# A two-layer hybrid trunk in float32: the S5 mixer's output products issued for two steps together, in four column groups

## The chip, the cores and the metric

The kernel runs on one core of a Trainium2 chip. The metric is the device time of one execution in microseconds (us), the median of three runs. A program that reads the hardware profile gives one profiled execution as a trace; its times count from the start of its span.

## The reference

One sequence of 256 positions, width 2048, two layers. Each layer normalises, scales and shifts by a modulation vector, projects to four head groups, mixes, projects back, and adds with a gate; then an MLP with squared ReLU.

```python
mod = c_act @ ada_w[l] + ada_b[l]
sh1, sc1, gt1, sh2, sc2, gt2 = split(mod, 6)
a = rms_norm(h, norm1_g[l]) * (1 + sc1) + sh1
proj = a @ w_in[l]                      # columns of S5, retention, window, latent attention
mixed = concat([y_s5, y_ret, y_swa, y_mla]) @ w_out[l]
h = h + gt1 * mixed
a = rms_norm(h, norm2_g[l]) * (1 + sc2) + sh2
h = h + gt2 * (square(relu(a @ mlp_w1[l])) @ mlp_w2[l])
```

The S5 mixer has 32 groups of 16 channels and 64 complex modes each: a linear recurrence over the positions, then

```python
y = einsum('bsgp,ghp->bsgh', st_r, c_re) - einsum('bsgp,ghp->bsgh', st_i, c_im) + d_skip * uf
z = gelu(y)
return z * sigmoid(z @ glu_w + glu_b)
```

## The kernel before, in words

Weights arrive as a stream of items of 256 rows by 512 columns (a few are narrower) by DMA on SyncE's queue (`pump_dma`, line 324). Each item is split into a high and a low part: ScalarE casts it to `wH`, VectorE makes the rest `wL` (`prep`, line 335). TensorE makes three products for each pair of tiles, high by high, high by low and low by high, so an item is 12 to 24 instructions. A list (`make_plan`, line 82) sets the order of the items; the items of the modulation (`ap`) go to TensorE directly, as products of 32 columns in four column groups (`pe_ap`, line 456).

The mixers run in the background of that stream. Each is a Python generator (`s5` at line 1310, `mla` for latent attention at 908, `swa` for the window at 858, `ret` for retention at 1054). After each piece of an item `step` (line 395) lets them advance in turn until what they emitted in this step is above a share of an engine's time (`BUD`, line 238), counted by estimates; S5 goes first. A generator that needs tiles or banks of PSUM waits until enough are free (`g_slots`, line 277, and `g_banks`), with 31 tiles and 8 banks in all. All engines take their instructions in the order in which this code emits them. All products stand under line 225 in the trace, since a helper records them, so the names of tiles tell them apart: `w<-` and `p<-` are general tiles and banks.

S5 takes its 16 sets of 128 modes two at a time, in eight steps `p`. A step reads the input's products from two banks, turns them into a rotating frame, scans both halves of the sequence on VectorE, and turns the states back: four results for each of two sets, in the tiles `W[2]` and `W[3]`. Then eight output products follow: four terms (real and imaginary part, two frames) for each of the two sets `e`. A product is 128 modes by 32 channels on 256 positions, and the 32 channels of set `i` stand in column group `32 * (i % 4)` of the bank `yp`. Two steps fill the four column groups of a bank, an even step the first two and an odd step the other two; then VectorE adds the skip term.

At the head of the output product `hload` and `ysplit` (line 708) wait for latent attention, the first of the four mixers that the output product takes, by `need`: the generators go on with no item of the stream between them until it is done.

```python
P8 = W[2 + e].rearrange("p c (b t) -> p (c b) t", b=2)   # line 1396
...
yield from g_slots(4)                                     # line 1326
```

Of the kernel before, what the change touches and what calls it, by code (L numbers as in the profile page):

```python
# [36 lines left out]
# blocks of the first layer's input product that run in step over k while the modulation arrives  # L37
EARLY = ("U", "C", "K", "Q")
# order of the other blocks, and of the mixers' outputs (s5, retention, window, latent) in the output product
# [27 lines left out]
def _gap(l, f):  # L67
    """the norm ahead of a block, with products of the modulation to fill the tensor engine's wait"""
    g = _ap_sec(l, SH1 if f == 1 else SH2, [2, 3])
    p = g[:8] + [("sqfin",)] + g[8:13] + [("norm", l, f)]  # L70
    if f == 1:
        p += [("start", l), ("lim", 6, 3)]
    p.append(("aquad", l, f, 0))
    return p + g[13:] + [("crepfree",)]


# halves of a quad of the normed input, ahead of which item of the block they are made
# [102 lines left out]
# columns of the constant array  # L180
# [30 lines left out]
class Meter:  # L211
    """An engine whose emitted work is counted, so that background work can be spread evenly."""
# [18 lines left out]
def trunk_kernel(ctx: ExitStack, tc: tile.TileContext, A, out):  # L231
    nc = tc.nc
    V, ACT, GP = Meter(nc.vector, 0.07, 1.04e-3), Meter(nc.scalar, 0.12, 0.83e-3), nc.gpsimd
    PE = Meter(nc.tensor, 0.05, 1.5e-3)

    NHL, NS, LA = 3, 31, 4
    # work that each slot of the stream may bring in, in us of vector, scalar and tensor engine, by layer
# [123 lines left out]
    def prep_real():  # L361
        """the next item that the scalar and vector engines prepare"""
# [5 lines left out]
    # items behind the next norm are not prepared ahead of it  # L368
    wall, w, k = {}, len(data_idx), len(data_idx)
    for it in reversed(PLAN):  # L370
# [3 lines left out]
        elif it[0] == "norm":  # L374
            w = k
# [19 lines left out]
    def step():  # L395
        """one slot: background generators advance until the slot's share of an engine is used up"""
# [84 lines left out]
    def ap_cols():  # L481
        """the row of 512 sums, four partial sums to a column, turned into four columns"""
# [29 lines left out]
    nst = {"acc": None, "pb": None}  # L512

    def sq_add(sq, w):
        """adds the squares of w chunks to the running sum over features"""
# [7 lines left out]
    def sq_fin():  # L523
        """the sum over partitions"""
# [30 lines left out]
    def aquad_a(l, f, q):  # L555
        """a = rstd * h * g * (1 + scale) + shift in two parts, the shortest way to the first chunks"""
# [23 lines left out]
    def aquad_half(l, f, q, c, stage):  # L580
        """the same for two chunks, in three stages that run apart"""
# [31 lines left out]
    def fm(acc, n, k0, first, last, xH, xL, w=512, wo=0, ng=4):  # L613
        """acc[bank][:, 256*...] += W.T @ x over the two k-chunks of item n; x as four-chunk tiles."""
# [39 lines left out]
    def pe_in(n, it):  # L654
        _, l, b, kq, hf = it
        # at the start, with all blocks in progress at once, two of them are summed up in SBUF
# [61 lines left out]
    def evict_half(l, gate, nb, acc, b):  # L718
        """h += gate * acc for two chunks, as soon as their bank is complete"""
# [100 lines left out]
    def softmax4(pv, sv, mask, scale, sink):  # L820
        """sv = softmax over the free axis of scale * (pv + mask), with an optional sink logit"""
# [20 lines left out]
    def transposed(views, nk):  # L842
        """[128 keys, 4 heads, 128 queries] per block of keys"""
# [796 lines left out]
```

## Time and profile before

| | |
|---|---|
| three runs | 2373.75, 2376.07, 2376.28 us |
| median | 2376.07 us |
| the profiled execution | span 2373.1 us; no other time of it is kept |
| instructions | 42933 |
| granted TensorE clock, mean | 0.991 of full speed |
| TensorE busy | 2303.7 us, 97% |
| VectorE busy | 1523.9 us, 64% |
| ScalarE busy | 1038.2 us, 44% |

Busy times are sums over the whole span; stages differ. The median of the runs is 3.0 us above the profiled span. The first layer's mixers stand between about 170 and 410 us, the second layer's between about 1290 and 1540 us. A product's row in the timeline has the time from its start until its end as modelled; products overlap, so the distance between starts is what one costs TensorE. The chain of waits follows the work that ended last back from its end.

### The profile page before, as it was taken

Reading aid. Unit: us, or ns where it says so; the run is one execution under the profiler, and the core shown is the slowest. Engines: PE = TensorE matmul, PEld = TensorE weight load, DVE = VectorE, ACT = ScalarE, POOL = GpSimd, SP = SyncE. Lnnn points to the kernel's source line nnn. Section 1 sums busy time; section 2 is a strip of 40 time slices with the busy share of each in tenths; the row PEclk is TensorE's granted clock in tenths of the full one; section 3 lists DMA queues with packets and bytes.
Section 4 is the critical chain, followed back from the end, with each engine's and each line's share of the span. In section 5 each row is a group of like instructions: output and inputs, shape, how many; then the busy total and the mean of one; then the engine's idle time right before and its main releaser. Section 6 shows DMA issues by size and latency. Waiting matters only on the chain.

```text
span 2373.1 us, 42933 instructions
## 1 busy us (share of the span) xinstructions
PE 2303.7 (97%) x17610; PEld 2092.8 (88%) x17610; DVE 1523.9 (64%) x2532; ACT 1038.2 (44%) x1330; POOL 31.8 (1%) x51
## 2 busy tenths in 40 slices
PE   6999999999999999999999889999999999999997
PEld 3675457989999999999988757898999999999997
DVE  4847774666666677788877986576444445555555
ACT  2343234554444444434445346445444444343444
POOL 0000000000000000000000000000000000000000
PEclk9999999999999999999999999999999999999999
DMA  9985786777888889988976224877555556676730
GB/s 379 408 309 190 272 305 262 249 286 258 273 275 282 273 295 322 319 320 284 323 278 245 98 69 145 299 269 289 183 201 182 194 191 211 238 233 231 237 126 36
DMA packets 161077, 583.65 MB, mean 246 GB/s; under 512 B 18240, under 2 KB 18400, under 8 KB 160880
## 3 DMA queue, kind: packets, MB, share of 16 engines
q1 hardware_dynamic: 156240, 563.80, 67.2%
q0 software_dynamic: 4640, 17.11, 2.0%
q8 instruction: 138, 2.26, 0.4%
q14 instruction: 59, 0.48, 0.1%
HBM read 576.64 MB, written 4.19 MB: 245 GB/s over the span
## 4 chain that ended last, share of the span: by engine, by line
PE 90%; DVE 5%; DMA 3%; ACT 1%; issue 1%; SPq 0%; POOL 0%; DVEq 0%; POOLq 0%; ACTq 0%
PE p L225 90%; DVE w L225 3%; DMA w<-in_stream_dram 3%; DVE wL L225 1%; ACT wH L225 0%; ACT w L225 0%; DVE s5i L225 0%; DVE nacc L225 0%; DVE aL L225 0%; ACT aH L225 0%; POOL mss L925 0%; SPq L306 0%; DVE ndg L225 0%; ACT L225 0%; ACT apev L225 0%
## 5 line engine op out<-in xcount | busy, mean ns | idle before, releaser
L225 PE MATMUL p<-aH,wH 128*128 128x256 f32 x4896 | 1393.7, 285 | 8.6 <-ACT aH L225 5.4
L225 PE MATMUL p<-aH,wL 128*128 128x256 f32 x4896 | 1388.3, 284 | 3.2 <-DVE wL L225 3.2
L225 PE MATMUL p<-aL,wH 128*128 128x256 f32 x4896 | 1388.3, 284 | 1.8 <-DVE aL L225 1.8
L225 DVE TENSOR_TENSOR wL<-w,wH 128x1024 fp32r<-128x1024 f32 (+1 forms) x688 | 833.4, 1215 | 734.9 <-ACT wH L225 723.1
L225 ACT CAST wH<-w 128x1024 fp32r<-128x1024 f32 (+1 forms) x688 | 712.5, 1039 | 928.5 <-PE p L225 845.5
L225 PEld LDWEIGHTS p<-aH,wH 128*128 128x128 f32 x4896 | 942.2, 192 | 25.4 <-ACT aH L225 7.8
L225 PEld LDWEIGHTS p<-aH,wL 128*128 128x128 f32 x4896 | 942.2, 192 | 3.8 <-DVE wL L225 3.8
L225 PEld LDWEIGHTS p<-aL,wH 128*128 128x128 f32 x4896 | 942.3, 192 | 2.6 <-DVE aL L225 2.4
L225 PE MATMUL p<-w,w 128*32 128x512 f32 (+5 forms) x1464 | 251.2, 508 | 12.3 <-DVE w L225 10.1
L225 DVE CUSTOM_DVE_ANT_0 w<-w,w 128x1024 f32<-128x1024 f32 x192 | 233.8, 1218 | 0.0
L225 PEld LDWEIGHTS p<-w,w 128*32 128x32 f32 (+3 forms) x1464 | 97.8, 134 | 110.0 <-issue 57.5
L225 PE MATMUL p<-wH,aH 128*128 128x512 f32 (+1 forms) x320 | 128.4, 401 | 5.9 <-ACT wH L225 5.9
L225 PE MATMUL p<-wL,aH 128*128 128x512 f32 (+1 forms) x320 | 118.9, 372 | 0.5 <-DVE wL L225 0.5
L225 PE MATMUL p<-wH,aL 128*128 128x512 f32 (+1 forms) x320 | 118.5, 370 | 0.0
L225 PEld LDWEIGHTS p<-wH,aH 128*128 128x128 f32 x320 | 60.8, 190 | 43.6 <-issue 22.1
L225 ACT ACTIVATE w<-w 128x1024 f32<-128x1024 f32 (+3 forms) x82 | 67.1, 823 | 55.1 <-DVE w L225 50.2
L225 ACT COPY w<-p 128x512 f32<-128x512 f32 (+1 forms) x80 | 45.6, 586 | 101.5 <-PE p L225 100.3
L225 DVE TENSOR_TENSOR aL<-w,aH 128x1024 fp32r<-128x1024 f32 (+2 forms) x86 | 72.2, 847 | 12.9 <-ACT aH L225 12.9
L225 PEld LDWEIGHTS p<-wH,aL 128*128 128x128 f32 x320 | 60.8, 190 | 11.0
L225 DVE TENSOR_TENSOR w<-w,w 128x512 f32<-128x512 f32 (+4 forms) x132 | 65.9, 526 | 6.2 <-ACT w L225 4.0
L225 PEld LDWEIGHTS p<-wL,aH 128*128 128x128 f32 x320 | 60.9, 190 | 9.8 <-DVE wL L225 1.4
L225 ACT ACTIVATE w<-p 128x512 f32<-128x512 f32 x68 | 40.6, 598 | 43.6 <-PE p L225 43.5
(153 smaller groups left out, 786.8 us busy)
## 6 DMA issues: line engine op xcount, KB each, us to landing
w<-in_stream_dram SPq DMA_DIRECT2D x1056, 512.0 KB, 4.9
w<-in_stream_dram SPq DMA_DIRECT2D x16, 320.0 KB, 9.5
w<-in_w_uq_dram POOLq DMA_DIRECT2D x6, 384.0 KB, 6.1
w<-in_xT_dram SPq DMA_DIRECT2D x4, 512.0 KB, 7.4
w<-in_glu_w_dram POOLq DMA_DIRECT2D x4, 512.0 KB, 5.6
w<-in_xT_dram POOLq DMA_DIRECT2D x4, 512.0 KB, 7.4
w<-in_c_dram POOLq DMA_DIRECT2D x4, 512.0 KB, 6.6
hs<-w POOLq DMA_DIRECT2D x4, 512.0 KB, 3.9
```

The lines of the kernel that those rows point to most:

```text
L225: return f(out, *a, **k)
```

## The change

S5 holds six tiles instead of four: the results of an even step go to `W[2]` and `W[3]`, those of an odd step to `W[4]` and `W[5]`. An even step emits no output products. The odd step takes a bank and emits the sixteen products of both steps: for each of the four terms the four sets, which go to four column groups. The rest of the text's difference is comments that were left out.

```diff
-        yield from g_slots(4)
-        W = [slot([128, 4, 256]) for _ in range(4)]
+        yield from g_slots(6)
+        W = [slot([128, 4, 256]) for _ in range(6)]
...
-                P8 = W[2 + e].rearrange("p c (b t) -> p (c b) t", b=2)
+                P8 = W[2 + 2 * (p % 2) + e].rearrange("p c (b t) -> p (c b) t", b=2)
...
-            if p % 2 == 0:
+            if p % 2 == 1:
+
                 yield from g_banks(1, 1)
                 yp = bank()
-            for n, (m, src) in enumerate(((0, 0), (0, 3), (1, 2), (1, 1))):
-                for e in range(2):
-                    i = 2 * p + e
-                    p0, cs, o = 32 * (i % 4), slice(32 * i, 32 * i + 32), 256 * (n == 3)
-                    PE.matmul(yp[p0:p0 + 32, o:o + 256], lhsT=C[:, m, cs], rhs=W[2 + e][:, src, :],
-                              start=n in (0, 3), stop=n in (2, 3), tile_position=(0, p0))
-            if p % 2 == 1:
+                for n, (m, src) in enumerate(((0, 0), (0, 3), (1, 2), (1, 1))):
+                    for e in range(4):
+                        i = 2 * p - 2 + e
+                        p0, cs, o = 32 * e, slice(32 * i, 32 * i + 32), 256 * (n == 3)
+                        PE.matmul(yp[p0:p0 + 32, o:o + 256], lhsT=C[:, m, cs], rhs=W[2 + e][:, src, :],
+                                  start=n in (0, 3), stop=n in (2, 3), tile_position=(0, p0))
                 yield
```

Since tiles, banks and counted time decide where each generator goes on, the other mixers' instructions move too. Three places show it. First TensorE in the first layer, ahead of the first output product. Before, the last products of S5's gate, the window's sums (`64x512`) and transposes of softmax results stand there:

```order
L225 MATMUL p_3107<-w_3153,w_110 32x512 x2
L225 MATMUL p_3107<-w_3157,w_110 32x512 x2
L225 MATMUL p_3257<-kc,apev 128x1 x4
L225 MATMUL p_3272<-w_3186,w_1516 64x512
L225 MATMUL p_3272<-w_3193,w_1516 64x512
L225 MATMUL p_3276<-kc,w_3059 128x128 x4
L225 MATMUL p_3283<-kc,w_3097 128x128 x2
L225 MATMUL p_3283<-kc,w_3098 128x128 x2
```

With the change, some rows after the scores of the second half of latent attention, these rows stand there (`w_3083` and `w_3084` are the retention queries and keys, `w_3107` and `w_3108` softmax results of the window):

```order
L225 MATMUL p_3241<-kc,apev 128x1 x4
L225 MATMUL p_3236<-w_3078,w_3074 128x256 x2
L225 MATMUL p_3236<-w_3078,w_3075 128x256 x2
L225 MATMUL p_3261<-kc,w_3083 128x128 x4
L225 MATMUL p_3285<-kc,w_3083 128x128 x4
L225 MATMUL p_3298<-w_3084 128x256
L225 MATMUL p_3298<-w_3084 128x128
L225 MATMUL p_3303<-kc,w_3107 128x128 x2
L225 MATMUL p_3303<-kc,w_3108 128x128 x2
L225 MATMUL p_3308<-w_3084 128x256
L225 MATMUL p_3308<-w_3084 128x128
```

The scores of latent attention and all of retention's heads have come ahead of the first output product; before, the scores stood among the input products and the heads among the output products.

Second, ScalarE's queue at the same place, with the change (`sxd` and `sxm` are sums and maxima of a softmax, `w_3209` and `w_3210` scores of latent attention):

```order
L225 ACTIVATE w_1477<-p_3236,s5d 128x256 x2
L225 COPY w_3084<-p_3261 128x4x128
L225 ACTIVATE w_3107<-w_3107,sxd 128x256 x2
L225 ACTIVATE w_3108<-w_3108,sxd 128x256 x2
L225 ACT_TABLE_LOAD
L225 ACTIVATE w_3209,sxd<-w_3209,sxm 128x256 x2
L225 ACTIVATE w_3210,sxd<-w_3210,sxm 128x256 x2
L225 COPY w_3084<-p_3285 128x4x128
L225 ACTIVATE w_3209<-w_3209,sxd 128x256 x2
L225 ACTIVATE w_3210<-w_3210,sxd 128x256 x2
L225 COPY w_3328<-p_3303 128x512
```

and before, where the queue ends in the cast of latent attention's result (`aH`):

```order
L225 ACTIVATE w_3097<-w_3097,sxd 128x256 x2
L225 ACTIVATE w_3098<-w_3098,sxd 128x256 x2
L225 COPY w_1712<-p_3272 64x4x128
L225 COPY w_3281<-p_3276 128x512
L225 COPY w_3288<-p_3283 128x512
L225 COPY w_3295<-p_3290 128x512
L225 COPY w_2803<-p_3297 128x4x128
L225 COPY w_2803<-p_3303 128x4x128
L225 CAST aH_3324<-w_2803 128x1024
```

A softmax of latent attention, with its table load, now stands between the two copies of the retention queries.

Third, TensorE in the second layer, inside the input product of the window's queries, with the change:

```order
L225 MATMUL p_14043<-aL_13291,wH 128x256
L225 MATMUL p_14043<-aH_13290,wL 128x256
L225 MATMUL p_14243<-w_13284,w_14149 128x256
L225 MATMUL p_14243<-w_13285,w_14149 128x256
L225 MATMUL p_14243<-w_13286,w_14149 128x256
L225 MATMUL p_14042<-aH_13375,wH 128x256
L225 MATMUL p_14042<-aL_13376,wH 128x256
```

Before, the same three products of latent attention's queries stand in the product of the retention queries, 180 instructions of the stream later:

```order
L225 MATMUL p_14398<-wH,aL_13481 128x512
L225 MATMUL p_14710<-w_14598,w_13736 64x512
L225 MATMUL p_14715<-w_13282,w_14208 128x256
L225 MATMUL p_14715<-w_13283,w_14208 128x256
L225 MATMUL p_14715<-w_13284,w_14208 128x256
L225 MATMUL p_14397<-wH,aH_13480 128x512
```

The other five groups of three, the key and value products and the first scores of latent attention have moved with them.

## Rows read from the trace of the kernel before

**Rows 1.** The page: span and instructions, and busy time of each engine.
```profile
span 2373.1 us, 42933 instructions
...
PE 2303.7 (97%) x17610; PEld 2092.8 (88%) x17610; DVE 1523.9 (64%) x2532; ACT 1038.2 (44%) x1330; POOL 31.8 (1%) x51
```
**Rows 2.** Chain that ended last, 170 to 420: start, us, what, instructions.
```profile
292.68 84.15 PE p L225 x434
...
385.28 1.05 ACT aH L225
...
387.64 32.48 PE p L225 x253
```
**Rows 3.** The same chain, 1280 to 1520.
```profile
1392.10 107.66 PE p L225 x506
...
1500.39 1.28 ACT L225
```
**Rows 4.** Busy time by stretch: length, busy by engine, granted clock, DMA share, GB/s.
```profile
1295.00:1392.00 97.00, 80.15 (x532) 62.98 (x531) 85.94 (x240) 35.26 (x68) 3.35 (x3) 0.95 0.23 79
1392.00:1500.00 108.00, 107.90 (x508) 77.74 (x509) 76.02 (x179) 57.90 (x115) 4.22 (x8) 1.00 0.43 153
293.00:371.00 78.00, 78.00 (x409) 43.40 (x406) 49.62 (x140) 32.04 (x65) 1.06 (x2) 0.97 0.71 258
1380.00:1390.00 10.00, 7.24 (x19) 4.63 (x20) 6.48 (x22) 4.55 (x11) 0.00 (x0) 0.51 0.15 52
```
**Rows 5.** Timeline, one burst of S5's output products: start, us, engine, instructions.
```profile
307.63 0.40 PE L225 MATMUL p<-wH,aL 128*128 128x512 f32 x1
...
307.96 1.44 PEld L225 LDWEIGHTS p<-w,w 128*32 128x32 f32 x16 [0.36 <-issue]
307.96 1.92 PE L225 MATMUL p<-w,w 128*32 128x256 f32 x16
...
309.81 0.50 PE L225 MATMUL p<-wH,aH 128*128 128x512 f32 x1
```
**Rows 6.** Timeline, the modulation's products: two items together, and one alone.
```profile
350.74 1.06 PE L225 MATMUL p<-w,w 128*32 128x512 f32 x8
...
356.75 1.05 PE L225 MATMUL p<-w,w 128*32 128x512 f32 x4
```
**Rows 7.** Timeline, other mixers on TensorE: scores, gate, column sums, a retention head.
```profile
352.36 0.70 PE L225 MATMUL p<-krT,w 64*128 64x256 f32 x2
352.99 0.70 PE L225 MATMUL p<-w,w 128*128 128x256 f32 x2
...
360.59 1.89 PE L225 MATMUL p<-w,w 128*128 128x256 f32 x8
...
377.49 1.05 PE L225 MATMUL p<-kc,apev 128*128 128x1 f32 x8 [0.73 <-ACT apev L225]
...
1513.21 0.92 PE L225 MATMUL p<-w 64*128 64x256 f32 x4
```
**Rows 8.** Timeline, TensorE's first products behind the first layer's input product.
```profile
370.95 5.80 PE L225 MATMUL p<-w,w 128*128 128x256 f32 x32
```
**Rows 9.** ScalarE: one exponential, table load, four scalings (timeline), and copies (by form).
```profile
360.36 0.49 ACT L225 ACTIVATE w<-w,sxm 128x256 f32<-128x256 f32 x1
...
361.95 1.28 ACT L225 ACT_TABLE_LOAD   x1
...
378.06 1.70 ACT L225 ACTIVATE w<-w,sxd 128x256 f32<-128x256 f32 x4
...
L225 ACT COPY w<-p 128x512 f32<-128x512 f32 x72 | 40.9, 587 | 89.1 <-PE p L225 87.9 <-DVE aL L225 0.6
```
**Rows 10.** Timeline, the second layer's product after a long wait of TensorE.
```profile
1380.22 0.79 PE L225 MATMUL p<-wH,aH 128*128 128x512 f32 x1 [5.91 <-ACT wH L225]
```
**Rows 11.** Timeline, three products of latent attention's queries and the one behind them.
```profile
1407.89 1.46 PE L225 MATMUL p<-w,w 128*128 128x256 f32 x6
1408.99 0.58 PE L225 MATMUL p<-wH,aH 128*128 128x512 f32 x1
```

## The prediction

> **What bounds the kernel now.** I read the page first, then the chain of work that ended last in the two stretches that hold an S5 mixer, then the busy time by stretch, then single bursts in the timeline. The page [rows 1]: TensorE is busy 97% of a span of 2373.1 us. A kernel like this gets shorter only by TensorE work that disappears or by TensorE idle time that closes. The chains say where TensorE is the limit. In the first layer it carries the chain for 84.15 us from 292.68, and after one ScalarE cast at 385.28 again from 387.64 [rows 2]; between 267 and 292.7 the chain is VectorE's. In the second layer TensorE has it for 107.66 us from 1392.10 and hands over at 1500.39 to a table load [rows 3]; ahead of that, from 1295, VectorE has it. The stretches agree [rows 4]: from 1295 to 1392 VectorE is busy 85.94 of 97 us and TensorE only 80.15, from 1392 to 1500 TensorE 107.90 of 108 and VectorE 76.02; from 293 to 371 TensorE 78.00 of 78, VectorE 49.62. So TensorE time saved between 1295 and 1392 buys nothing, saved behind 1392 or behind 293 it is the kernel's.
>
> **The change, part by part.** *The bursts.* One S5 step issues 8 output products, 16 instructions, to two column groups. In the timeline [rows 5] the 16 start at 307.96 and the next product of the stream at 309.81; the last product before started at 307.63. Products of that stream follow at 0.23 us, so a burst costs 309.81 - 307.63 - 0.23 = 1.95 us. 1.85 us for 16 instructions is about eight steps of 0.216: two instructions share a step already. Four groups are seen elsewhere: the modulation's products write 32 columns each too, and eight of their instructions (two items, four column groups) take 1.06 us, four (one item, two groups) 1.05 us [rows 6]. Twice the groups, same time. Those stream 512 columns, the S5 products 256, so I take 0.216 us for a set of four and 1.95 us for a burst of 32. Bounds: 1.95 (as with the modulation) and 3.7 (no gain over pairs, 32 instructions at two to a step and one change of form). Sixteen bursts become eight: 8 x 1.95 = 15.6 us of TensorE work less.
>
> A row that bears on the weights: the 16 loads of that burst are spread over 1.44 us at the same time as its products [rows 5], although all use the same 128 rows. The Trainium skill (TensorE: Matmul & The Clock Gate, Part 3, "What overlaps and what doesn't") says that a load overlaps running products only when the row group differs; by that rule these loads would stand between the products. The row speaks against it, and by it a burst of 32 would cost 2.9 us more (32 loads at 1.44/16).
>
> *What else moves.* The work of the mixers is dealt out in steps by emitted engine time, with slots and banks as tokens. S5 now wants 6 tiles instead of 4, an even step emits no products, and the bank of the sums is held inside the odd step only. The order shows what follows: in both layers S5 keeps its pace, but the latent and retention work lands elsewhere. I sum TensorE time by place, with prices from rows: a score product every 0.63 us, so a block of eight 5.0, half a gate product of S5 (four products) 1.89, column sums 1.05, one retention head 0.92 [rows 7]. Small scores are half as wide, 0.4 each and 3.2 a block, by an estimate from the same rows.
>
> *First layer.* (a) Up to the last quarter of the retention queries the work is 1 us more, in VectorE's stretch: 0. (b) From there to the end of the input product (288 to 371) four bursts become two (-3.9), the latent scores of the second half (-5.0) go behind it, half a gate product too (-1.9), and small scores, a wide product and transposes (an estimate of 4.4) go ahead of it: -15. VectorE, busy near its limit up to 340, keeps some: I take **-13** (bounds -6 and -15).
>
> (c) Then the output product must wait for latent attention. Before, the time from the last input product's end to the first output product is 370.95 [rows 8] to the end of the cast, 386.3 [rows 2]: 15.4 us. Now the second half's scores stand inside it. I follow the order by durations. TensorE: gate half 1.9, modulation 1.0, scores 5.0, modulation 1.0, gate half 1.9, column sums 1.05, gate half 1.9: 13.7. ScalarE, in its queue: two sigmoids (0.9), copy 0.59, four scalings 1.70, table 1.28, four exponentials of 0.49, and only then the copy of the second half of the retention queries, 0.59 [rows 9]: 20.8. All retention heads wait for that copy, and TensorE idles from 14.4 to 20.8. Then four heads 3.7, sixteen transposes and the products of three mixers behind them, an estimate of 7.4: 32. A copy, four squares and the cast (1.05) [rows 2] close it: about 35 us. Difference **+20**. The rows also show what such an idle time does to the clock: after TensorE had stood idle for 5.91 us up to 1380.22 [rows 10], the granted clock from 1380 to 1390 was 0.51 [rows 4], the lower of its two levels (1.2 GHz), and the product at 1380.22 took 0.79 us. I add **+2** for that (bounds 0 and 5). (d) Retention's heads and output products, which stood inside the output product, have moved ahead: **-6.9** (four heads 3.4 to 3.7, small products 2.8, transposes 0.7, the last two by estimate). First layer: -13 + 20 + 2 - 6.9 = **+2**.
>
> *Second layer.* The latent projections move ahead by some 20 weight items, from TensorE's stretch into VectorE's: six groups of three products, each 1.1 us (1407.89 to 1408.99) [rows 11], and by estimate from such rates transposes 1.0, key and value products 2.8, small scores 3.2: 13.7 us. (e) 1295 to 1392: TensorE gets +13.7 and loses three bursts, 5.9; its 17 us of idle time take the 7.8. VectorE gets six operations of the queries' rotary, an estimate of 2.2 us: **+2.7** with what the tighter coupling costs (bounds 0 and 10). (f) 1392 to 1500: -13.7, one burst less (-1.95), three to four retention heads come in (+3.4): **-12.2**. TensorE then needs 96 us against VectorE's 78, so it stays the bound. (g) Behind 1505 those heads and small products are gone: **-5.0**. The end at 1500 (table, two activations, cast) does not hang on latent attention and stays. Second layer: 2.7 - 12.2 - 5.0 = **-14.5**.
>
> DMAs: no transfer is added or taken out; two more tiles held by S5 delay some weight issues by one item, which the prefetch covers except perhaps between 325 and 371, inside (b)'s bound. VectorE's and ScalarE's instructions are the same in number but for one table load.
>
> Sum: +2 - 14.5 = **-12.5 us** on the span of 2373.1. The median of the runs, 2376.07, is 3 us above that span; the same difference on it gives **2364 us**. A measurement of this kernel can tell about 0.2%, 4.75 us, from no change.
>
> **Rivals.**
> *Only the bursts count* (0.20): the delay (c) is hidden or (b) comes in full, and the two layers net to the 15.6 us less work, a little more where idle time closes: 2360. For it: TensorE is busy 97%. Against: one third of the bursts stand in VectorE's stretches.
> *VectorE holds both stretches* (0.12), the slower side: in the first layer VectorE (or the weights' DMA) does not let the input product end earlier, so (b) gives 4 instead of 13, while (c) costs its 20 to 22; in the second the 7.8 us in (e) come on top of VectorE's chain. Sum: -4 + 22 - 6.9 + 10 - 12.2 - 5.0 = +4, and +9 if (f) also loses half to VectorE: 2377 to 2385. It decides from the point where (b) is below 7. For it: VectorE is at 89% from 1295 on [rows 4]. Against: 49.62 of 78 from 293 on.
> *The groups do not overlap by fours* (0.07): each burst keeps two to a step, 1.75 us more on the six bursts outside VectorE's stretch, -12.5 + 10.5 = -2: 2374. Against it: rows 6.
> *The loads are exposed* (0.03): 2.9 us more on six bursts, 2381. It is what the rule of the skill quoted above would do here; the trace does not agree with that rule.
>
> **How the numbers follow.** The forecast's own case has 0.58; the likeliest time is its 2364, its own range 2354 to 2373 (drain (c) as little as 27 us, TensorE's work alone, gives -8; (b), (e) and the clock at their bad ends give +9). Low end: 2353, just under that. High end: 2376, which takes in the third rival and leaves out most of the second and the fourth, some 0.15, and 0.05 lie under the low end. Faster by over 0.2%: 0.48 of the first, 0.20 of the second, 0.01 of the groups' case: 0.69. Within 0.2%: 0.08 + 0.07 + 0.06: 0.21. Slower: 0.02 + 0.05 + 0.03: 0.10.
>
> **What the profile after would show.** Eight bursts of 32 instructions that start in sets of four, 0.22 us apart, 1.8 to 2.0 us each. In the first layer the last input product ends near 358, the first output product starts near 393, with some 6 us of idle TensorE ahead of the first retention head, named as waiting for ScalarE. In the second layer the chain leaves VectorE near 1397 and the stretch to the output product is about 12 us shorter. I am wrong if pairs are seen in the bursts, if the first layer's output product starts later than 400, or if VectorE keeps the chain of the second layer beyond 1410.

## The result and the profile after

The change makes the kernel slower: 2395.8 us (median of 2393.88 to 2404.28) against 2375.47 us, with a recorded ratio of 1.0092 and a 95% interval of 1.0079 to 1.0105. The forecast was 2364, in a range of 2353 to 2376.

The page after, beside [rows 1]:

```profile
span 2395.7 us, 42934 instructions
...
PE 2306.0 (96%) x17610; PEld 2100.2 (88%) x17610; DVE 1523.9 (64%) x2532; ACT 1040.7 (43%) x1331; POOL 30.9 (1%) x51
```

TensorE has the same 17610 instructions and is busy 2.3 us *longer*, although sixteen bursts have become eight. Its idle time is 2395.7 - 2306.0 = 89.7 us, and was 69.4.

A burst where nothing waits, from TensorE's timeline after (start, us, engine, instructions):

```profile
1365.71 1.93 PE L225 MATMUL p<-w,w 128*32 128x256 f32 x32
1367.57 0.39 PE L225 MATMUL p<-aH,wH 128*128 128x256 f32 x1
```

32 instructions hold TensorE from 1365.71 to 1367.57, 1.86 us; 16 took 1.85 [rows 5]. Their weights load at the same time:

```profile
1365.70 1.45 PEld L225 LDWEIGHTS p<-w,w 128*32 128x32 f32 x32
```

Where nothing waits, the part that the change is about does what was forecast. Four of the eight bursts are like this one: their first and last starts lie 1.55 us apart. In the other four these starts lie 2.36 (first layer), 7.33, 7.41 and 6.11 us apart (second layer). These bursts wait in their middle for results of VectorE, and those of the second layer then run at the lower clock; two of them are shown below.

The first layer's drain, TensorE's timeline after, to be read against [rows 2, 8] (the last figure is the idle time and what ended it):

```profile
364.71 3.51 PE L225 MATMUL p<-w,w 128*128 128x256 f32 x18
...
385.00 1.64 PE L225 MATMUL p<-w 64*128 64x256 f32 x4 [5.98 <-ACT w L225]
...
404.12 0.38 PE L225 MATMUL p<-aH,wH 128*128 128x256 f32 x1 [3.34 <-ACT aH L225]
```

and ScalarE in it:

```profile
379.38 1.71 ACT L225 ACTIVATE w<-w,sxd 128x256 f32<-128x256 f32 x4
381.12 1.28 ACT L225 ACT_TABLE_LOAD   x1
...
384.39 0.56 ACT L225 COPY w<-p 128x512 f32<-128x512 f32 x1
```

The first retention head (385.00) waits 5.98 us for the copy of the second retention queries, which stands behind four scalings, a table load and four exponentials. Behind that wait TensorE has the lower of its two clock levels, 0.50 of full speed (columns as in [rows 4]):

```profile
385.00:394.00 9.00, 8.99 (x34) 7.13 (x35) 2.40 (x8) 3.16 (x8) 0.00 (x0) 0.50 0.02 2
```

The first output product starts at 404.12, before at 386.3.

The chain after, where the input product of the first layer should have come sooner (start, us, what):

```profile
296.62 3.48 DMA w<-in_stream_dram
...
326.05 7.10 DMA w<-in_stream_dram
333.23 1.05 ACT wH L225
334.30 1.23 DVE wL L225
...
343.27 34.89 PE p L225 x187
```

Before, TensorE had the chain without a break from 292.68 [rows 2]. Now two weights arrive late, 10.6 us of the chain, and TensorE has it for good only from 343.27.

The second layer, busy time by stretch after; the columns are those of [rows 4]:

```profile
1412.00:1526.00 114.00, 100.22 (x463) 69.44 (x462) 77.14 (x182) 55.09 (x103) 3.68 (x7) 0.96 0.46 166
```

Before, the same part of the stream, from 1392 to 1500, had TensorE busy 107.90 of 108 [rows 4]. It lost its latent projections, as forecast, and takes longer: 13.8 us are idle. The waits of TensorE in it:

```profile
PE p L225 <- DVE w L225: 8.3, 3, 4.0
PE p L225 <- ACT w L225: 5.2, 3, 3.4
```

One of the three waits for VectorE, in the timeline of all engines:

```profile
1425.75 0.41 ACT L225 ACTIVATE w<-w,sxm 128x128 f32<-128x128 f32 x1 [5.11 <-DVE sxm L225]
...
1427.10 0.63 PE L225 MATMUL p<-w,w 128*32 128x256 f32 x6
...
1428.83 1.03 ACT L225 CAST wH<-w 128x1024 fp32r<-128x1024 f32 x1
...
1429.89 1.22 DVE L225 TENSOR_TENSOR wL<-w,wH 128x1024 fp32r<-128x1024 f32 x1 [2.28 <-ACT wH L225]
...
1431.04 1.28 DVE L225 TENSOR_TENSOR w<-w,w 128x512 f32<-128x512 f32 x2
...
1431.78 3.37 PE L225 MATMUL p<-w,w 128*32 128x256 f32 x26 [4.04 <-DVE w L225]
...
1435.07 0.77 PE L225 MATMUL p<-wH,aH 128*128 128x512 f32 x1
```

The stretch behind the wait (columns of [rows 4]), then the second layer's last burst in TensorE's timeline:

```profile
1431.80:1435.00 3.20, 3.20 (x26) 1.08 (x26) 1.66 (x2) 0.10 (x1) 0.00 (x0) 0.57 0.60 193
...
1470.44 0.63 PE L225 MATMUL p<-w,w 128*32 128x256 f32 x6
1473.57 3.42 PE L225 MATMUL p<-w,w 128*32 128x256 f32 x26 [2.50 <-DVE w L225]
```

Read the first of the two views from its end. The burst stops after 6 of 32 instructions, because VectorE has not made the last set's results (1431.04). These stand behind the low part of a weight (1429.89), that waited 2.28 us for ScalarE's cast (1428.83), the cast stands behind latent attention's small exponentials (1425.75), and these waited 5.11 us for VectorE's maxima. Three queues in order, each waiting for another. The remaining 26 instructions then take 3.3 us, some 0.41 for a set of four and not 0.22: the granted clock is 0.57 there. The last burst stops at the same place for 2.50 us. So 6.5 of the 13.8 us of idle time stand in the middle of two bursts. Before, TensorE was idle for 0.1 us of the stretch [rows 4]. The chain after shows one more thing on the way, a late weight (start, us, what), and TensorE has the chain for good only from 1493.33:

```profile
1476.42 7.29 DMA w<-in_stream_dram
...
1493.33 32.84 PE p L225 x130
```

### The profile page after: what moved, and what is told of

Read it like the earlier page. It is cut to its first block, busy times and chain, and to the rows that moved or that the text cites. A ratio compares the mean times of both kernels' runs of the same rounds, so it can differ in the third digit from the quotient of the medians.

```text
span 2395.7 us, 42934 instructions
## 1 busy us (share of the span) xinstructions
PE 2306.0 (96%) x17610; PEld 2100.2 (88%) x17610; DVE 1523.9 (64%) x2532; ACT 1040.7 (43%) x1331; POOL 30.9 (1%) x51
## 4 chain that ended last, share of the span: by engine, by line
PE 84%; DVE 8%; DMA 3%; ACT 3%; issue 1%; SPq 0%; POOL 0%; DVEq 0%; POOLq 0%; ACTq 0%
PE p L225 84%; DVE w L225 5%; DMA w<-in_stream_dram 3%; DVE wL L225 2%; ACT w L225 1%; ACT wH L225 1%; DVE s5i L225 0%; ACT aH L225 0%; ACT L225 0%; DVE f L225 0%; DVE aL L225 0%; DVE nacc L225 0%; ACT rjk L225 0%; POOL mss L925 0%; DVE ndg L225 0%
## 5 line engine op out<-in xcount | busy, mean ns | idle before, releaser
L225 PE MATMUL p<-w,w 128*32 128x512 f32 (+4 forms) x1464 | 243.3, 526 | 21.8 <-DVE w L225 15.2
L225 PEld LDWEIGHTS p<-w,w 128*32 128x32 f32 (+2 forms) x1464 | 95.3, 137 | 113.7 <-issue 59.5
L225 PEld LDWEIGHTS p<-wL,aH 128*128 128x128 f32 x320 | 61.7, 193 | 13.7 <-DVE wL L225 5.0
L225 PEld LDWEIGHTS p<-wH,aL 128*128 128x128 f32 x320 | 61.4, 192 | 11.1
```

The costliest lines, as they stand in the source:

```text
L225: return f(out, *a, **k)
```

## The experiments

My theory at the start (A): the loss comes from when other work is dealt out, since the even step no longer takes a bank and no longer counts products. Its rivals: the two more tiles that S5 holds (B), and the sixteen products behind one wait (C).

In the tables below "first" and "second" are how much later the stream stands behind each layer's mixers than in the trace of before: the start of one product of the stream (at 436.41 and at 1554.46 us before), in the profiled execution of each kernel; "second" has the first taken off. Executions of one kernel differ by some us (those of the kernel before by up to 6.4 within one series), so a difference of a few us in these columns means little by itself. The time is the median of the timed runs. The ratio, with its 95% interval, is the recorded one against executions of the kernel before that were timed along with the run; it differs from the ratio of the two medians by up to 0.0006.

| run | tiles of S5 | bank, count in the even step | time, us | ratio | first, us | second, us |
|---|---|---|---|---|---|---|
| the change | 6 shared | no, no | 2395.8 | 1.0092 (1.0079, 1.0105) | +11.4 | +11.2 |
| six_tiles, old bursts | 6 shared | as before | 2404.9 | 1.0126 (1.0109, 1.0143) | +16.0 | +10.9 |
| bank_and_count | 6 shared | yes, yes | 2402.7 | 1.0114 (1.0099, 1.0129) | +16.8 | +10.7 |
| bank_only | 6 shared | yes, no | 2411.2 | 1.0151 (1.0136, 1.0167) | +20.0 | +17.3 |
| count_only | 6 shared | no, yes | 2395.8 | 1.0088 (1.0073, 1.0103) | +12.1 | +11.1 |
| own_tiles_both | 4 shared, 2 own | yes, yes | 2373.2 | 0.9990 (0.9981, 1.0000) | -2.5 | +1.0 |
| own_tiles | 4 shared, 2 own | no, no | 2395.0 | 1.0082 (1.0067, 1.0097) | +9.4 | +11.4 |
| own_tiles_count | 4 shared, 2 own | no, yes | 2384.1 | 1.0040 (1.0025, 1.0055) | +7.1 | +3.0 |
| own_tiles_both_pairs | 4 shared, 2 own | yes, yes | 2375.6 | 0.9998 (0.9988, 1.0008) | +2.2 | +1.0 |

**Which part of the change.** Beside the bursts three things changed at once: the tiles S5 holds, the place where a bank is taken, and the place where sixteen products are counted. First, the tiles alone, in the kernel before:

```diff
-        yield from g_slots(4)
-        W = [slot([128, 4, 256]) for _ in range(4)]
+        yield from g_slots(6)
+        W = [slot([128, 4, 256]) for _ in range(6)]
...
-                P8 = W[2 + e].rearrange("p c (b t) -> p (c b) t", b=2)
+                P8 = W[2 + 2 * (p % 2) + e].rearrange("p c (b t) -> p (c b) t", b=2)
...
-                    PE.matmul(..., rhs=W[2 + e][:, src, :], ...)
+                    PE.matmul(..., rhs=W[2 + 2 * (p % 2) + e][:, src, :], ...)
```

> The kernel before, with six tiles for S5 and the results of odd steps in the last two; the eight products follow each step as before. Theory A (it is the time when other work is dealt out that costs: the even step no longer holds a bank and no longer counts products): little changes, 2374 to 2382 us, the first layer within 5 us of before at its first output product and the second layer's stretch to the output product within 4 us. Theory B (two more tiles held starve the other mixers and the weights): most of the loss is here already, 2390 to 2398. Theory C (sixteen products behind one wait make TensorE stand for VectorE): nothing here, 2374 to 2380.

Then the change with bank and count where they were:

```diff
-            if p % 2 == 1:
+            if p % 2 == 0:
                 yield from g_banks(1, 1)
                 yp = bank()
+                PE.t += 8 * (0.05 + 1.5e-3 * 256)
+            else:
+                PE.t -= 8 * (0.05 + 1.5e-3 * 256)
```

> The change, but the even step takes and holds the bank as before, and its eight products are counted at its place (and not in the odd step), so that the other mixers' work falls exactly as with six tiles alone. Theory A: the burst's saving is seen at last, four bursts of 1.95 us outside the stretches of VectorE, some 8 us under six tiles alone: 2366 to 2374 us. Theory B: 2383 to 2393. Theory C: the bursts still wait in their middle, 2390 to 2398.

bank_only has these lines without the two of `PE.t`; count_only has the two of `PE.t`, and takes the bank in the odd step.

> The change, with the bank taken and held by the even step, and the products counted where they are issued. By the order this puts the first layer's work as in the run with bank and count, and leaves the second layer as in the change. Theory A: the loss of the first layer (11.4 us) goes, that of the second (11.2 us) stays: 2378 to 2388 us. Theory B and theory C: as the change, 2390 to 2398.

> The change, with the even step's products counted at its place, and the bank taken in the odd step. By the order this leaves the first layer as in the change and puts the second nearly as in the run with bank and count. Theory A: the loss of the first layer (11.4 us) stays, the second layer gains some 4 us on before instead of losing 11.2: 2378 to 2388 us. Theory B and theory C: as the change, 2390 to 2398.

Theory A fell at once: six tiles with the old bursts lose 29 us, more than the whole change. Theory C has no support as the cause of the loss, since the run with old bursts loses as much as the others. Bursts do wait in their middle, but the old form does too, once the order is another. In six_tiles, in the first layer:

```profile
351.42 3.22 PE L225 MATMUL p<-w,w 128*32 128x256 f32 x18 [3.48 <-DVE w L225]
```

The burst at that place waits 3.69 us in bank_and_count. Theory B was right on which part loses, not on how much: six_tiles, bank_and_count and bank_only lie above every range that a theory had given for them. The bursts' form is worth next to nothing here. In the traces of six_tiles and bank_and_count each of TensorE's 1706 instructions outside the stream's products and the bursts stands behind the same product of the stream, and the two runs are 2.2 us apart with overlapping intervals.

Bank and count are no fixed costs. With six shared tiles the change loses the same when the count goes back to its old place (count_only), and 15.4 us *more* when the bank does (bank_only).

**S5's tiles from memory of its own.** If taking two tiles from the others is the harm, two new ones must cure it:

```diff
-        yield from g_slots(6)
-        W = [slot([128, 4, 256]) for _ in range(6)]
+        yield from g_slots(4)
+        W = [slot([128, 4, 256]) for _ in range(4)]
+        W += [sp.tile([128, 4, 256], F32, tag=f"own{i}", name=f"own{i}") for i in range(2)]
...
-                nst["acc"] = sm.tile([128, 256], F32, tag="nacc", name="nacc", bufs=1)
+                nst["acc"] = sm.tile([128, 256], F32, tag="ndg", name="nacc", bufs=1)
...
```

The other lines that make room let retention's `rjk` use the tag `ndg`, and four tables of S5 the tags `mkr` and `krT`. own_tiles_both has bank and count as above, own_tiles_count the count alone.

> The change with bank and count as in the even step of before, and S5's two more tiles taken from memory of its own, not from the 31 that all share (room is made by letting small tiles of the norm, of retention's sums and of S5's tables share theirs). The order of all work is then that of before, but for the bursts. Theory B (the tiles taken from the other mixers and the weights are the whole loss): the burst's saving remains, four bursts of 1.95 us outside VectorE's stretches, 7.8 us off before: 2364 to 2371 us, no burst waits in its middle in the second layer behind 1392. Theory C (sixteen products behind one wait): bursts still wait in their middle for 3 to 5 us and cost more than they save: 2376 to 2392. A new one, D (TensorE is never short enough for the products to matter: its saved time turns into idle time with a lower clock behind it): within 3 us of before.

> The change as it stands, with two tiles of its own. The bank and the count still move other work: latent attention some 180 instructions of the stream ahead in the second layer. Theory B: the loss is gone, and what moves is worth what the prediction gave it or nothing: 2358 to 2374 us. If moving the work is itself harmful (theory A in what is left of it), the second layer keeps a loss of 7 to 15 us: 2376 to 2386. Theory C: 2380 to 2396.

> Two tiles of its own, the products of the even step counted there, but the bank taken in the odd step. The second layer is by the order as in the run with both, the first as in the run with tiles alone. Theory B: 2362 to 2372, and its difference to the run with both is the first layer's part of the bank, its difference to tiles alone the second layer's part of the count. Theory C: 2376 to 2392.

own_tiles_both is the change with the order of before: by its trace none of the 1706 instructions stands behind another product of the stream. It is level with before or a little faster, 2.3 us less, of an interval that reaches 1.0000, as theory D had it. So the room-making lines cost nothing that is seen. With tiles of its own the change still loses 19.5 us once bank and count move (own_tiles), so theory B is not enough: the lost tiles are one of three ways to disturb the order. Moving the bank costs the first layer 9.6 us (7.1 against -2.5, own_tiles_count against own_tiles_both); moving the count too costs the second layer 8.4 (11.4 against 3.0). With tiles of its own the count was not moved alone but for a run with a hold, further below. The bank in the even step, which gains 10.9 us here, cost 6.9 with shared tiles (bank_and_count against count_only): what a move is worth depends on the rest of the order.

The first layer's loss of own_tiles is not the drain of the change. Its stream stands 6.9 us ahead of before at the product at 300.69 before, 5.0 behind at the last of the input product, and 5.6 behind at the first output product: it is lost inside the input product, with no tile taken from the weights.

The page of own_tiles_both says where the bursts' gain went:

```profile
span 2371.5 us, 42925 instructions
...
PE 2294.7 (97%) x17610; PEld 2093.5 (88%) x17610; DVE 1523.4 (64%) x2532; ACT 1038.0 (44%) x1330; POOL 31.8 (1%) x51
```

TensorE is busy 9.0 us less than before [rows 1] and idle 76.8 us, 7.4 more: most of the saved time has become idle time. And it shows what the change lost, since both have the same bursts: 24.2 us of span are 11.3 us more busy time for the same instructions and 12.9 us more idle time. The first fits a lower clock on the same work: the mean granted clock is 0.981 after and 0.986 here, 0.5% of 2300 us. Before it was 0.991, so a lower clock may also take part of what the bursts save.

**Four column groups or two.** In own_tiles_both_pairs the sixteen products go out as eight for sets 0 and 1, then eight for 2 and 3:

```diff
-                for n, (m, src) in enumerate(((0, 0), (0, 3), (1, 2), (1, 1))):
-                    for e in range(4):
+                for h2, n, m, src in [(h2, n, m, src) for h2 in range(2) for n, (m, src) in enumerate(...)]:
+                    for e in (2 * h2, 2 * h2 + 1):
```

> As the run with both, but the sixteen products of a burst go out as two times eight: the four terms for sets 0 and 1 (two column groups), then for sets 2 and 3. Same place, same order of all else. If four column groups share a step of TensorE as two do, a burst of 32 instructions takes 3.5 us here instead of 1.8, and the time is 5 to 9 us above the run with both (four bursts outside VectorE's stretches). If the groups bring nothing, the two runs agree within 2 us.

A burst behind the same product of the stream, in the timeline of TensorE (`own` are the tiles of sets 2 and 3), first of own_tiles_both:

```profile
304.88 0.41 PE L225 MATMUL p<-w,w 128*32 128x256 f32 x2
304.89 0.41 PE L225 MATMUL p<-own,w 128*32 128x256 f32 x2
305.12 0.39 PE L225 MATMUL p<-w,w 128*32 128x256 f32 x2
...
306.74 0.50 PE L225 MATMUL p<-wH,aH 128*128 128x512 f32 x1
```

then of own_tiles_both_pairs:

```profile
308.52 1.27 PE L225 MATMUL p<-w,w 128*32 128x256 f32 x10
309.42 0.41 PE L225 MATMUL p<-own,w 128*32 128x256 f32 x2
309.63 0.39 PE L225 MATMUL p<-w,w 128*32 128x256 f32 x2
309.66 0.39 PE L225 MATMUL p<-own,w 128*32 128x256 f32 x2
...
311.27 0.50 PE L225 MATMUL p<-wH,aH 128*128 128x512 f32 x1
```

1.86 us against 2.75, not 3.5: the second eight start 0.90 us after the first, while half of those are still to run. So order in four groups is worth 0.9 us a burst against two halves. The two runs stand 2.4 us apart, with intervals that overlap a little; the traces differ by 4.7 us, all in the first layer, but the profiled execution of own_tiles_both_pairs is the slowest of its ten. The expected 5 to 9 us were too many by the burst that was mis-sized.

**Is it scarcity?** Two theories were left: tiles are scarce (B, for the weights or for the other mixers), or the kernel before is fitted to its numbers and nearly any other order loses (T). tiles33 gives the kernel *before* two tiles more, with room made by the lines that own_tiles_both has too:

```diff
-    NHL, NS, LA = 3, 31, 4
+    NHL, NS, LA = 3, 33, 4
```

> The kernel before with 33 tiles for all instead of 31, nothing else (room is made as for S5's own tiles). If tiles are scarce and their lack holds work up (theory B), two more let other mixers and weights come earlier: 2360 to 2373 us. If the kernel before is fitted to its numbers of tiles, banks and counts, so that nearly any other order loses (theory T), it is slower although nothing is taken away: 2380 to 2400.

The other three are six_tiles with the reserve that a waiting party leaves untouched two lower while S5 holds its six: for the fetch of weights, for the mixers, for both (`more[0]` is 2 in that time):

```diff
-        while st["dma"] < len(data_idx) and len(raws) < lim["n"] and len(slots) > lim["res"]:
+        while st["dma"] < len(data_idx) and len(raws) < lim["n"] and len(slots) > lim["res"] - more[0]:
...
-        while len(slots) < n + reserve:
+        while len(slots) < n + reserve - more[0]:
```

> The kernel before with six tiles for S5, but while S5 holds them the fetch of weights may go two tiles deeper into the reserve, so that it stops where it did before. The other mixers still find two tiles fewer. If it is the late weights that cost (theory B1), most of the 29 us of six tiles alone comes back: 2376 to 2388. If it is the other mixers' wait for tiles (B2), or a loss by any other order (T), it stays at 2396 to 2410.

> The kernel before with six tiles for S5, but while S5 holds them the other mixers may go two tiles deeper into the reserve, so that they wait as they did before. The weights find two tiles fewer. B2 (the mixers' wait for tiles costs): 2376 to 2388. B1 (late weights) or T: 2396 to 2410.

> The kernel before with six tiles for S5, and both the weights and the other mixers go two tiles deeper while S5 holds them, so that all waits for tiles stop where they did before from then on; the wait for the six tiles themselves is left. B1 or B2: 2374 to 2384. T: the order still is not that of before (the latent attention of the second layer some 4 us of TensorE work further ahead), 2388 to 2410.

| run | time, us | ratio | first, us | second, us |
|---|---|---|---|---|
| tiles33 | 2407.4 | 1.0137 (1.0121, 1.0152) | +27.2 | +5.2 |
| six_weights | 2409.9 | 1.0148 (1.0133, 1.0163) | +23.0 | +11.8 |
| six_mixers | 2405.7 | 1.0130 (1.0115, 1.0145) | +21.8 | +9.2 |
| six_both | 2394.5 | 1.0085 (1.0069, 1.0102) | +6.4 | +9.2 |

More tiles and the room for them: 32 us slower, even past the range that theory T gave. Its first layer, busy time by stretch and TensorE's timeline:

```profile
385.00:399.00 14.00, 14.00 (x30) 7.22 (x30) 1.97 (x13) 0.00 (x0) 0.00 (x0) 0.50 0.20 75
...
410.89 5.23 PE L225 MATMUL p<-kc,w 128*128 128x128 f32 x20 [7.51 <-ACT w L225]
...
420.55 0.38 PE L225 MATMUL p<-aH,wH 128*128 128x256 f32 x1 [1.75 <-ACT aH L225]
```

A longer drain than after the change: TensorE works at a granted clock of 0.50 for 14 us, then waits 7.51 us for a softmax on ScalarE, and the output product starts at 420.55. B1 and B2 fall: neither party's old limit brings the loss back, and both together (six_both) still lose 19 us. Nor is it the count of displaced instructions: 500 of the 1706 stand behind another product of the stream than before in six_both, 406 in six_tiles, which loses more. Of the theories that were put up T is left, but not as "nearly any other order loses": in own_bank_late and the last two runs below instructions stand elsewhere than before, and none of the three is slower.

**The second layer's loss.** Here the prediction had put its gain. The runs below only hold back latent attention's projections in that layer until S5 begins step 5, which puts them near their old place:

```diff
             pbs = nxt
+            if p == 5:
+                ready["S5at", l] = True
...
         done.add(("CQ", l))
         yield from g_wait(2)
+        if l == 1:
+            yield from g_ready(("S5at", l))
```

> The change itself, with that one hold in the second layer. The first layer is untouched and keeps its 11.4 us. If the place of latent attention is what the second layer loses by: most of its 11.2 us go, 2384 to 2390. If not: 2394 to 2400.

> The change with S5's two tiles of its own, and in the second layer latent attention's projections held back until S5 begins its step 5 of 8, which puts them near their old place in the stream. Nothing else is changed. If the place of latent attention is what the second layer loses by (11 us between the run with own tiles and the one with count): 2382 to 2387 us. If it is something else in the uncounted even steps: 2392 to 2397. Theory T (nearly any other order loses) says only that the second layer stays above before: 2379 or more.

> Two tiles of its own, the bank taken in the even step, no count, and the hold of latent attention in the second layer. The first layer is by the order that of the run with both, 2.5 us before the kernel before. If latent attention's place decides the second layer: within 3 us of the run with both, 2371 to 2377. If not, the second layer loses 8 to 12 us: 2382 to 2388.

| run | time, us | ratio | first, us | second, us |
|---|---|---|---|---|
| change_late | 2386.0 | 1.0043 (1.0027, 1.0060) | +11.9 | -0.5 |
| own_tiles_late | 2391.5 | 1.0062 (1.0038, 1.0087) | +6.4 | +2.8 |
| own_bank_late | 2373.5 | 0.9984 (0.9975, 0.9993) | -6.5 | +1.0 |
| second_only_late | 2373.2 | 0.9991 (0.9982, 1.0000) | -1.3 | -2.4 |
| first_own_second_late | 2368.6 | 0.9971 (0.9962, 0.9981) | -5.9 | -3.1 |

One hold of one generator gives the change 9.8 us back, all of its second layer's loss. With the hold the count is of no weight either: own_bank_late has it moved, and its second layer stands where that of own_tiles_both does (+1.0). The stretch of change_late by busy time:

```profile
1412.00:1508.00 96.00, 94.79 (x477) 71.53 (x476) 69.89 (x170) 49.93 (x97) 4.22 (x8) 1.00 0.45 160
```

and its two bursts there, from the timeline:

```profile
1423.59 1.93 PE L225 MATMUL p<-w,w 128*32 128x256 f32 x32
...
1459.56 1.93 PE L225 MATMUL p<-w,w 128*32 128x256 f32 x32
```

TensorE is busy 94.79 of 96 at a granted clock of 1.00, and neither burst waits. own_tiles_late is unclear: its runs spread from 2384.0 to 2396.1, its trace (2382.2) says what was expected, its median does not.

**Both layers mended.** second_only_late leaves the first layer as it was before; first_own_second_late has there S5's own tiles and the bank in the even step. Both have the change, shared tiles and the hold in the second:

```diff
+        n_w = 6 if l else 4
+        yield from g_slots(n_w)
+        W = [slot([128, 4, 256]) for _ in range(n_w)]
+        if l == 0:
+            W += [sp.tile([128, 4, 256], F32, tag=f"own{i}", name=f"own{i}") for i in range(2)]
...
+            if p % 2 == 0 and l == 0 or p % 2 == 1 and l == 1:
                 yield from g_banks(1, 1)
                 yp = bank()
```

> The first layer as in the kernel before (four tiles, eight products after every step); the second layer with the change (six of the shared tiles, sixteen products in the odd step) and latent attention held back until step 5. By the trace of the run of the change with that hold, the second layer takes 4 to 5 us less than before: 2370 to 2374 us. If that gain came from the state in which the first layer left the queues, 2375 to 2380.

> The first layer with S5's two tiles of its own and the bank in the even step (2.5 to 6.5 us less than before in two traces), the second as in the run second_only_late (4 to 5 us less): 2364 to 2371 us if the two add up. Theory T allows any sum above that where the orders meet, 2372 to 2378.

The two add up: 2368.6 us, 7.1 less than the kernel before and 27 less than the change, with the change's bursts in both layers. The second layer's part is smaller than expected, 2.4 us in second_only_late and not 4 to 5. At the product at 1500.05 before, its stream is 8.8 us ahead, and 3.7 at the one at 1554.46; what it loses again behind 1500 was not followed. How much of the 7.1 us is the bursts' and how much the hold's is open: the hold was not tried with the bursts of before.

## Why the prediction was wrong

The prediction failed where it took TensorE for the bound of two stretches. The offsets in time of the same product of the stream, after against before, judge its steps:

- *The bursts, 1.95 us for 32 instructions*: right where nothing waits (1.86 us from start to the next product). The rival of groups that don't overlap by fours is out. The sum of 15.6 us has no term for bursts that wait in their middle, as three of the second layer's four do (up to 7.41 us from first to last start).
- *The loads*: the loads of those 32 instructions add nothing that is seen. The rule of the Trainium skill (TensorE: Matmul & The Clock Gate, Part 3, "What overlaps and what doesn't") would, by the prediction's estimate, have added 2.9 us. The trace does not agree with that rule for products of one row group in different column groups.
- *(a)* 0, measured -3.3 us up to the product at 300.69 before.
- *(b)* -13, bounds -6 and -15, measured -3.0: the last input product's end is 6.2 us sooner (364.71 against 370.95), 3.0 of it in this step. **This failed.** TensorE did not stay the bound: two weights came late, and the chain went over DMA, ScalarE and VectorE. The sentence on the DMAs said that "two more tiles held by S5 delay some weight issues by one item, which the prefetch covers except perhaps between 325 and 371". One of the late weights (296.62) lies outside that exception, the other (326.05) inside it. That the two tiles made them late is not shown: own_tiles, which takes none, loses more in this step.
- *(c)* +22 with the clock, measured 39.4 us against 15.4, +24.0: right, with the 6 us of idle TensorE (5.98) and the queue on ScalarE that was named.
- *(d)* -6.9, measured -6.3: right. First layer +11.4 instead of +2.
- *(e)* +2.7, bounds 0 to 10, measured +7.5: the size.
- *(f)* -12.2, measured +6.1. **This is the step that failed most.** "TensorE then needs 96 us against VectorE's 78, so it stays the bound": both numbers hold (94.79 in change_late, 77.14 after), the conclusion does not. Busy times were compared engine by engine, as if an engine below the other's sum were out of the way. With TensorE's work made small and latent attention's work moved ahead, the round of ScalarE's cast, VectorE's low part and S5's results, in queues in order, ends last, though no engine in it is full. After such a wait TensorE works at its lower clock for some microseconds (0.57 behind 1431.8), a cost that had been put at 2 us for the whole kernel. That the place of latent attention makes this round is shown by change_late, which moves it back and has TensorE busy again.
- *(g)* -5.0, measured -2.4. Second layer +11.2 instead of -14.5.

Of the prediction's own signs of being wrong two came: the first layer's output product starts later than 400 (404.12), and VectorE keeps a large part of the second layer's chain far beyond 1410, until TensorE has it from 1493.33. Two of its sums do not come out of their terms, without weight for the result: TensorE's work in (c) ends at 13.7 us, not 14.4, and the slower rival with half of (f) gives +10, not +9.

The slower rival had the first layer's half of the mechanism (the input product does not end earlier, (b) gives 4), and stopped at +9 because it gave VectorE's chain only half of (f). The prediction read the change as a sum of moved work. The runs show it as a new order: tiles, bank and count cost up to 29 us when they move, or bring some back, by what else has moved, and a gift of two tiles costs 32. What distinguishes the old order was followed at two places only: the short drain of the first layer, which is read from traces, and the place of latent attention in the second, which was tested. Why the old order is that good elsewhere, and why other orders lose in the first layer's input product, stays open.

## What to carry to other kernels

Where one program deals work out by counted time, tiles and banks, an edit that moves any of the three is a new schedule, and its cost is not the cost of the edit: first make the order equal, to see what the edit is worth (here 2.3 us, by its interval 0 to 4.5), then fit the order again (here some 5 us more). Work moved away from a stretch where an engine is full is a gain only if the next thing to end last there, here a round of three queues none of which is full, is shorter by as much. Idle time of a few microseconds on TensorE costs more than itself when the clock falls behind it, as after the wait of 5.98 us, with 0.50 granted over the next 9 us.

## What was not expected of the hardware

Products in other column groups start before the earlier ones are through their queue: in own_tiles_both_pairs the second half begins 0.90 us after the first, after four of its eight steps of 0.216 us, so that the 32 instructions take 2.75 us instead of twice 1.73. In the program all products of sets 0 and 1 stand ahead of those of sets 2 and 3, and yet a row of the latter starts at 309.42 and one of the former at 309.63. The Trainium skill (TensorE: Matmul & The Clock Gate, Part 3, "What overlaps and what doesn't") says that products start and end strictly in program order; these starts do not.

The same idle time does not always have the same price. Ahead of the first layer's output product TensorE waits 1.75 and 0.88 us in own_tiles_both; the two starts that the waits lead to lie 1.26 us apart, as they do before. TensorE's timeline and its busy time by stretch, before:

```profile
386.38 0.38 PE L225 MATMUL p<-aH,wH 128*128 128x256 f32 x1 [1.75 <-ACT aH L225]
387.64 0.39 PE L225 MATMUL p<-aL,wH 128*128 128x256 f32 x1 [0.88 <-DVE aL L225]
...
385.00:390.00 5.00, 2.74 (x20) 2.55 (x21) 1.23 (x1) 1.29 (x2) 0.00 (x0) 1.00 1.02 408
```

and in own_tiles_both, 5.1 us sooner:

```profile
381.27 0.38 PE L225 MATMUL p<-aH,wH 128*128 128x256 f32 x1 [1.75 <-ACT aH L225]
382.53 0.58 PE L225 MATMUL p<-aL,wH 128*128 128x256 f32 x1 [0.88 <-DVE aL L225]
...
380.00:385.00 5.00, 2.85 (x12) 2.65 (x13) 1.23 (x1) 1.19 (x2) 0.00 (x0) 0.66 1.02 408
385.00:390.00 5.00, 5.00 (x31) 5.00 (x30) 0.00 (x0) 1.33 (x2) 0.00 (x0) 0.65 1.03 411
```

The granted clock stays at 1.00 in the one and is 0.66 and 0.65 for ten microseconds in the other, which is at the lower of its two levels (1.2 GHz) for two thirds of them. It loses 2.6 of its 5.1 us there (at the product that starts at 392.71 before). What decides between the two was not tried.
